# Attention's order on four engines: drawn by a builder that keeps a clock for each engine and counts buffers, in place of fixed rates

## The chip, the core and the metric

One core of a Trainium2 chip runs one kernel. It has five engines that follow their own instruction queues, each strictly in order, and wait for each other through semaphores: TensorE (PE; the loading of its weights is shown apart, as PEld), VectorE (DVE), ScalarE (ACT), GpSimd (POOL) and SyncE (SP), which here issues nearly all transfers. The metric is device time in microseconds (us), the median of the runs.

## What is computed

One layer of a streaming encoder on 1024 frames of width 1024: three token mixers side by side, merged by sigmoid gates, then a gated feed-forward block with a convolution. The two mixers whose order changes are both softmax attention over the whole sequence, eight heads each, in query blocks of 128:

```python
def one_block(args):
    i, q_blk = args
    s = jnp.einsum('bqhd,bkhd->bhqk', q_blk, k).astype(jnp.float32) * scale
    p = jax.nn.softmax(bias_mask(i, s), axis=-1).astype(v.dtype)
    return jnp.einsum('bhqk,bkhd->bqhd', p, v)
...
hn = rms_norm(x, norm_mix_g[l])
u = hn @ w_in[l]
...
y_a = mla_branch(...) @ w_br_mla[l]
y_b = fox_branch(...) @ w_br_fox[l]
y_c = ssm_branch(...) @ w_br_ssm[l]
g = jax.nn.sigmoid(u_gate + b_gate[l]).reshape(Bsz, S, N_BRANCH, D_MODEL)
merged = g[:, :, 0] * y_a + g[:, :, 1] * y_b + g[:, :, 2] * y_c
```

"mla" heads have keys of 96, "fox" heads keys of 64 and a decay added to the scores; both masks are causal, so query block i needs i + 1 key blocks. The third mixer is a state-space scan (SSD). Of the input projection u, the part for the SSD's convolution (12 blocks of 128 columns) and for the gates (24 blocks) is not computed ahead: it is kept back as filling work for TensorE.

## The kernel before

The program runs in stages, each a stretch of code in which the tile framework places semaphores by what every instruction reads and writes: projections and norms (about 0 to 384 us), attention (to 898 us), the SSD (to 1092 us), the three branch projections and the merge, the output projection, and the feed-forward block, which takes the last third of the time. Every product is done as three fp32r matmuls of high and low parts, which is why "h" and "l" tiles go in pairs.

**Attention.** A unit is two query rows (blocks of 128 queries, i = 2 jp and 2 jp + 1) of one head: 16 heads times 4 units. For a row, TensorE writes the scores `s` (L1303; for fox heads a small mask matmul L1313 closes them), VectorE takes the negated row maximum `nmx` (L1314), ScalarE the exponential with its sum `pm`, `rs` (L1316), VectorE the reciprocal (L1320), GpSimd multiplies the row by it (L1321). Then, for every pair of key blocks, TensorE transposes up to four blocks of `pm` into PSUM (`tp`, L1379), ScalarE copies them out as `pth` (L1384), VectorE subtracts to get `ptl` (L1385), and TensorE multiplies both by the values `vv` into one half of the accumulator `o` (PV, L1344 to L1352). The last PV of a unit is the narrow one on the diagonal. After it ScalarE copies one part of the half out (`o1`, L1357) and VectorE adds the other (`o2`, L1362), which is then stored. Units take the two halves of `o` in turn; both halves are one tile of 128 x 512 values.

**Fill.** `all_fill` yields the kept-back projection in grains of six matmuls of 512 columns (L1181, tile `mm`); a block of 128 columns is two halves of 24 matmuls. All halves use one PSUM bank, which ScalarE empties (L1159 for a gate, L1186 for a convolution block). Weights of a block are loaded one block ahead and split by ScalarE (`wh`, L1123) and VectorE (`wl`, L1124). A convolution block is followed by a chain on GpSimd (L1145), VectorE (L1138, six taps; L1142, two outputs) and ScalarE (L1151). What attention does not use of the fill is spent in the SSD, whose own budget per step is `FILL_SSD`.

**Who sets the order.** Within attention only TensorE is ordered by hand (`manual_schedule` with one engine). A builder merges three streams: the scores of unit n, the transposes and PV of unit n - 2, and fill at a fixed rate (`FILL_ATT` times the other work). Non-PE instructions are emitted by `later(us, fn)` when a single clock, which counts only TensorE's work, has passed a guessed delay; the PV stays two transposed blocks behind (`PVLAG`). The order on ScalarE, VectorE and GpSimd is then chosen by the framework's own scheduler, but for fill's instructions, which `pin` keeps in program order.

```python
later(t0 + 0.15, lambda: V.reduce_max(nmx[:, 0:1], row, axis=AX, negate=True))
t1 = t0 + 0.4 + 0.135 * n
pl[0] = later(t1, lambda: A.activation(p_[:, 0:n * P], row, AF.Exp, ...))
```

**Behind the SSD.** For its last chunk (the eighth) VectorE finishes `y`, ScalarE squares it, GpSimd and VectorE take the root, ScalarE scales it (L1597), TensorE transposes it in two groups (`stp`, L1605), which ScalarE copies out (`yT`, L1606). The branch projection starts with the fox branch (`ybr`, L1725) on `ah` and `al`, the split attention output (L134 on ScalarE, L135 on VectorE), whose first split is held behind the scaling of the last chunk.

Of the kernel before, what the change touches and what calls it, by code (L numbers as in the profile page):

```python
# [42 lines left out]
def block_kernel(ctx: ExitStack, tc: tile.TileContext, x, positions, norm_mix_g, w_in, b_gate,  # L43
# [1032 lines left out]
    def later(us, fn):  # L1076
        h = [clk[0] + us, uid(""), fn]
        queue.append(h)
        return h
# [9 lines left out]
    def force(h):  # L1089
        if h is not None and any(e is h for e in queue):  # L1090
            run_until(h[0])

    class Ring:


        def __init__(self, pool, shape, dt, tag, bufs):
            self.a = (pool, shape, dt, tag, bufs)
            self.last = []

# [12 lines left out]
    pin = tc.keep_in_program_order  # L1112

    def fill_load(c0, now=False):
# [8 lines left out]
        later(4.0, lambda: pin(A.activation(h, raw, AF.Copy)))  # L1123
        rl[0] = later(5.3, lambda: pin(V.tensor_sub(l, raw, f32(h))))  # L1124
        return h, l, rl

    def conv_done(j, u, ul, t0):
        a, al = f_t4.get()
        t = [t0]

        def step(us, fn):
            h = later(t[0], fn)
            t[0] += us
            return h
# [6 lines left out]
        def out(c0, c1):  # L1141
# [4 lines left out]
                                          op0=ALU.mult, op1=ALU.add))  # L1146
# [3 lines left out]
        for c0, c1 in ((0, 512), (512, S)):  # L1150
            step(1.6, lambda c0=c0, c1=c1: pin(A.activation(u[:, c0:c1], a[:, c0:c1], AF.Tanh)))  # L1151
        step(1.1, out(0, 512))
        al[0] = step(1.0, out(512, S))
        ul[0] = step(0.0, lambda: SY.dma_start(xbc_d[j], u))
# [8 lines left out]
    def all_fill():  # L1163
# [5 lines left out]
        for n, (kind, j, c0) in enumerate(blocks):  # L1169
# [3 lines left out]
            force(rl[0])  # L1173
            u, ul = f_t4.get()
            for half in range(2):
                f_half[0] += 1
                ps, pl = f_ps[f_half[0] % len(f_ps)].get()
# [12 lines left out]
                pl[0] = later(wait + 1.4, fn)  # L1190
                if half == 1:
                    if kind == "c":
                        conv_done(j, u, ul, 2.2)
                    else:
                        ul[0] = later(wait + 2.0, lambda u=u, g=g_d[kind][j]: SY.dma_start(g, u))
                t_h = clk[0]
                yield 0.65 * grain[0]
                for _ in range(4):
                    if len(f_ps) == 1 and clk[0] - t_h < 1.5 + 0.65 * grain[0]:
# [6 lines left out]
    def advance(gen):  # L1206
        c = next(gen, None)
        if c is not None:
# [79 lines left out]
    def score_row(o, i, pn):  # L1288
        flush()
        n = i + 1  # L1290
        chunks = row_chunks(i)
        p_, _ = a_pm.get()
        nmx, _ = a_nmx.get()
        rs, rl = a_rs.get()
        qs = slice(i * P, i * P + P)
        ps, pl = a_s.get()
        z = 512 - chunks[0][1] if len(chunks) == 2 else 0
        row = ps[:, z:z + n * P]
        for ci, (a, b) in enumerate(chunks):
            w = max(b - a, 256)  # L1300
            last = ci == len(chunks) - 1
            for i_, (q_, k_) in enumerate(o.passes):
                T.matmul(ps[:, z + a:z + a + w], q_[:, qs], k_[:, a:a + w], start=i_ == 0,  # L1303
                         stop=(o.br == 0 or not last) and i_ == len(o.passes) - 1)
            c = len(o.passes) * w / 2400
            if not last:
                yield c
        pn.append((p_, rl))

        def finish(t0=0.0):  # L1310

            if o.br == 1:
                T.matmul(row[:, n * P - P:n * P], identb, mfox, start=False, stop=True)  # L1313
            later(t0 + 0.15, lambda: V.reduce_max(nmx[:, 0:1], row, axis=AX, negate=True))  # L1314
            t1 = t0 + 0.4 + 0.135 * n
            pl[0] = later(t1, lambda: A.activation(p_[:, 0:n * P], row, AF.Exp, bias=nmx[:, 0:1],  # L1316
                                                   accum_out=rs[:, 0:1]))

            def norm():
                V.reciprocal(rs[:, 1:2], rs[:, 0:1])  # L1320
                G.tensor_scalar(p_[:, 0:n * P], p_[:, 0:n * P], rs[:, 1:2], 0.0, op0=ALU.mult, op1=ALU.add)  # L1321
# [888 lines left out]
```

## Time and profile before

| | |
|---|---|
| runs | 1999.05, 2001.5, 2002.47 us; median 2001.5 |
| profiled execution | 2000.52 us, its span 1998.8 us, granted clock 1.0 |
| attention, first fill matmul to last PV | 384.3 to about 898 us |
| SSD, to the first branch matmul | about 898 to 1092 us |
| fill matmuls in attention, in the SSD | 1195 and 533 of 1728, from the order of the instructions |

How to read it: PE's busy share counts pipelined matmuls whose ends are modelled, so two matmuls overlap in the rows; what one costs is the distance from its start to the next start. A view of waits names the engine that sat idle, the line it then ran, and the engine and line whose result came last.

### The profile page before, as it was taken

What the parts mean: (1) busy time and instruction counts of PE and PEld (TensorE: products, weight loads), DVE (VectorE), ACT (ScalarE), POOL (GpSimd) and SP (SyncE); (2) the same over time, 40 slices, a digit from 0 to 9 for tenths busy, and PEclk for the clock granted to TensorE, in tenths of its full rate; (3) what the DMA queues carried; (4) which work ended last, traced back from release to release, by engine and by line L of the source; (5) the groups of instructions that cost most, each with busy time, mean ns of one, the idle gap of its engine ahead of it and who ended that gap; (6) DMA issues with size and microseconds to landing.
All of it is one profiled execution on the core that took longest, in us unless ns stands there. A gap on an engine that the chain in (4) does not pass through costs nothing.

```text
span 1998.8 us, 28317 instructions
## 1 busy us (share of the span) xinstructions
PE 1975.3 (99%) x10185; PEld 1678.4 (84%) x10185; DVE 1340.1 (67%) x2153; ACT 929.3 (46%) x1650; POOL 660.1 (33%) x636
## 2 busy tenths in 40 slices
PE   8999999999999999999999999999999999999999
PEld 7989888888888888888888788888878888888887
DVE  7777567266656666656885476568998777665655
ACT  5555323255555555547775132225454445444432
POOL 5133322022222223213331262100664544523665
PEclk9999999999999999999999999999999999999999
DMA  5166857543535445427654786433332211249575
GB/s 179 52 195 211 276 178 226 166 126 105 139 114 146 116 124 134 127 78 238 182 193 137 258 278 211 139 125 104 107 95 85 76 61 49 79 154 336 195 259 193
DMA packets 278262, 312.15 MB, mean 156 GB/s; under 512 B 19197, under 2 KB 209289, under 8 KB 278122
## 3 DMA queue, kind: packets, MB, share of 16 engines
q1 hardware_dynamic: 278120, 310.35, 49.7%
q8 instruction: 80, 1.31, 0.3%
q14 instruction: 60, 0.49, 0.1%
q10 hardware_dynamic: 2, 0.00, 0.0%
HBM read 217.17 MB, written 93.13 MB: 155 GB/s over the span
## 4 chain that ended last, share of the span: by engine, by line
PE 88%; DVE 4%; DMA 3%; issue 2%; ACT 1%; POOL 1%; SPq 1%; ACTq 0%; DVEq 0%; POOLq 0%
PE mm L1181 18%; PE dn L2157 10%; PE fx L798 9%; PE ybr L1725 7%; PE ua L1816 6%; PE uc L1816 5%; PE ud L1816 4%; PE wo L1861 4%; PE s L1303 4%; PE tp L1379 3%; PE ub L1816 2%; PE fxv L188 2%; PE py L1570 1%; PE o L1352 1%; PE ckv L517 1%
## 5 line engine op out<-in xcount | busy, mean ns | idle before, releaser
L1321 POOL TENSOR_SCALAR pm<-pm,rs 128x128 f32<-128x128 f32 (+7 forms) x128 | 115.8, 906 | 403.0 <-DVE rs L1320 378.7
L1181 PE MATMUL mm<-hnh,wh 128*128 128x512 f32 x576 | 237.9, 413 | 0.0
L1181 PE MATMUL mm<-hnh,wl 128*128 128x512 f32 x576 | 225.9, 392 | 0.0
L1181 PE MATMUL mm<-hnl,wh 128*128 128x512 f32 x576 | 225.6, 392 | 0.0
L2157 PE MATMUL dn<-dr,dr 128*128 128x512 f32 x592 | 182.3, 389 | 0.0
L1385 DVE TENSOR_TENSOR ptl<-tp,pth 128x512 fp32r<-128x512 f32 (+1 forms) x160 | 98.7, 631 | 70.5 <-ACT pth L1384 69.9
L2157 PEld LDWEIGHTS dn<-dr,dr 128*128 128x128 f32 x592 | 111.1, 188 | 23.0
L1384 ACT ACTIVATE pth<-tp 128x512 fp32r<-128x512 f32 (+1 forms) x160 | 85.4, 555 | 94.5 <-PE tp L1379 94.3
L1181 PEld LDWEIGHTS mm<-hnh,wl 128*128 128x128 f32 x576 | 108.2, 188 | 24.8
L1316 ACT ACTIVATE pm<-s,nmx 128x128 f32<-128x128 f32 (+7 forms) x128 | 94.6, 741 | 71.8 <-DVE nmx L1314 71.3
L1314 DVE TENSOR_REDUCE nmx<-s 128x1 f32<-128x128 f32 (+7 forms) x128 | 95.3, 751 | 48.8 <-PE s L1303 26.9
L1181 PEld LDWEIGHTS mm<-hnl,wh 128*128 128x128 f32 x576 | 108.8, 189 | 15.9
L1181 PEld LDWEIGHTS mm<-hnh,wh 128*128 128x128 f32 x576 | 108.7, 189 | 16.1 <-DVE o L1362 0.2
L2157 PE MATMUL dn<-dr 128*128 128x512 f32 x296 | 115.2, 389 | 0.0
L135 DVE TENSOR_TENSOR dr<-dr,dr 128x1024 fp32r<-128x1024 f32 x52 | 71.5, 1382 | 52.1 <-ACT dr L134 48.1
L1725 PE MATMUL ybr<-ah,wl 128*128 128x512 f32 x256 | 99.7, 389 | 0.7 <-DVE wl L135 0.7
L1725 PE MATMUL ybr<-ah,wh 128*128 128x512 f32 x256 | 99.7, 389 | 0.3 <-ACT wh L134 0.3
L1725 PE MATMUL ybr<-al,wh 128*128 128x512 f32 x256 | 99.8, 390 | 0.0
L134 ACT ACTIVATE dr<-dr 128x1024 fp32r<-128x1024 f32 x52 | 55.1, 1061 | 71.7 <-PE dn L2157 51.0
L134 ACT ACTIVATE wh<-wr 128x1024 fp32r<-128x1024 f32 (+1 forms) x40 | 35.1, 877 | 97.8 <-PE ybr L1725 44.3
L1379 PE MATMUL tp<-ident,pm 128*128 128x128 f32 x576 | 79.1, 273 | 0.0
L135 DVE TENSOR_TENSOR wl<-S,wh 128x1024 fp32r<-128x1024 f32 x42 | 63.1, 1503 | 23.3 <-ACT wh L134 23.3
(528 smaller groups left out, 5705.3 us busy)
## 6 DMA issues: line engine op xcount, KB each, us to landing
dr<-act_d SPq DMA_DIRECT2D x99, 256.0 KB
wr<-in_w_in_dram SPq DMA_DIRECT2D x36, 512.0 KB
g_d<-t SPq DMA_DIRECT2D x24, 512.0 KB
gl<-g_d SPq DMA_DIRECT2D x24, 512.0 KB
wr<-in_ffn_w_up_dram SPq DMA_DIRECT2D x23, 512.0 KB
ws<-in_ffn_w_down_dram SPq DMA_DIRECT2D x22, 512.0 KB
wsum_d<-ws SPq DMA_DIRECT2D x22, 512.0 KB
act_d<-fa SPq DMA_DIRECT2D x22, 512.0 KB
```

The costliest lines, as they stand in the source:

```text
L134: i = A.activation(h, src, AF.Copy) if he is A else he.tensor_copy(h, src)
L135: return i, le.tensor_sub(l, src, f32(h))
L798: T.matmul(p, a(k), b(k), start=k == 0 and i == 0, stop=k == NK - 1 and i == 2)
L1181: T.matmul(ps, a[:, k, :], b[half][:, k, :], start=(k == 0 and i == 0), stop=(k == NK - 1 and i == 2))
L1314: later(t0 + 0.15, lambda: V.reduce_max(nmx[:, 0:1], row, axis=AX, negate=True))
L1316: pl[0] = later(t1, lambda: A.activation(p_[:, 0:n * P], row, AF.Exp, bias=nmx[:, 0:1], accum_out=rs[:, 0:1]))
L1321: G.tensor_scalar(p_[:, 0:n * P], p_[:, 0:n * P], rs[:, 1:2], 0.0, op0=ALU.mult, op1=ALU.add)
L1379: T.transpose(pt[:, off:off + P], pn[qi][0][:, k * P:k * P + P], ident)
L1385: pl[0] = later(cs + 0.6, lambda th=th, tl=tl, pt=pt, off=off: V.tensor_sub(tl[:, :off], pt[:, :off], f32(th[:, :off])))
L1725: T.matmul(pss[half], w_[:, k, :], a_[k][:, hs], start=k == 0 and i == 0, stop=k == nk - 1 and i == 2)
L1816: T.matmul(ps, a, b, start=first and n == 0, stop=n == 11, skip_group_check=not first)
L2157: T.matmul(ps[m], a[:, ts_], b[:, 512:], start=first_ and j == 0 and q == 0, stop=j == NFH - 1 and q == 2, skip_group_check=not first_)
```

## The change

It keeps all arithmetic and every number of instructions on each engine, and draws the order of attention anew. The builder now has a class `Task` (an engine, the time for which it blocks the engine, the time until its result is there, what it comes after, which buffers it takes) and a class `Sim`, with one clock for each of PE, ACT, DVE, POOL and the DMA queue. It places the task that can start first, an engine's ties by a rank; fill is put on TensorE when none of the three streams (PV before transposes before scores, `ORDER`) can start within `SLACK` of the end of the instruction before, or when fill is behind its share. A buffer's earlier owner must have been placed, and its end, plus `LATE`, counts. The costs are straight lines in the number of columns. Rows may now run as far ahead as the buffers allow (`pm` 8 buffers, was 6); the values need not be two blocks behind. A head's operands are loaded when the head two before it has ended. `manual_schedule` now holds PE, ACT, DVE and POOL, so their order in attention is the builder's, and `pin` does nothing there.

```diff
+    class Task:
+        def __init__(self, eng, cost, fn, after=(), est=0.0, order=(9, 0), rings=(), name=None):
+            self.eng, (self.pace, self.cost), self.fn = eng, cost, fn
...
-    pin = tc.keep_in_program_order
+    def pin(ins):
+        return ins if sim[0] is not None else tc.keep_in_program_order(ins)
...
-        later(4.0, lambda: pin(A.activation(h, raw, AF.Copy)))
-        rl[0] = later(5.3, lambda: pin(V.tensor_sub(l, raw, f32(h))))
+        i = later(4.0, lambda: pin(A.activation(h, raw, AF.Copy)), "A", (0.95, 1.06))
+        rl[0] = later(5.3, lambda: pin(V.tensor_sub(l, raw, f32(h))), "V", (1.13, 1.22), [i])
...
+    LATE = 0.09
+    class Sim:
...
+        def est(self, t):
+            if t.left:
+                return None
+            e = max([t.est] + [d.done + LATE for d in t.after])
+            for r, _ in t.rings:
+                if len(r.rel) >= r.bufs:
+                    o = r.rel[-r.bufs]
+                    if o.start is None:
+                        return None
+                    e = max(e, o.done + LATE)
+            return e
...
+        def pick_pe(self):
+            f = self.free["P"]
...
+            if t0 is not None:
+                behind = self.used < self.total * min(1.0, self.worked / self.work) + self.lead
+                if fe is None or (fe > t0 + 0.02 if behind else t0 < fe + SLACK):
+                    e = min((e for e in c if e[0] <= t0 + 0.02), key=lambda e: e[1])
+                    return e[0], e[2], e[3]
+            if fe is not None:
+                return fe, None, None
...
-    FILL_ATT = 1.08
+    ORDER = "VTS"
+    SLACK = 0.15
...
-        a_pm = Ring(atp, [P, S], F32, "pm", 6)
-        a_th, a_tl = (Ring(atp, [P, 512], F32R, n, PVLAG + 2) for n in ("pth", "ptl"))
+        PM, TH = 8, 4
...
-        with tc.manual_schedule(engines={mybir.EngineType.PE}):
...
-                merge(st, FILL_ATT * share)
...
+            m = Task("V", (d - 0.09, d), f_max, [ss[-1]], 0.0, (2, seq))
+            e = Task("A", (d - 0.115, d), f_exp, [m], 0.0, (2, seq), [(r_pm, last_t)])
+            rc = Task("V", (0.07, 0.16), lambda: V.reciprocal(r.rs[:, 1:2], r.rs[:, 0:1]), [e], 0.0, (1, seq))
+            d = 0.27 + 0.00084 * cols
+            r.norm = Task("G", (d - 0.025, d), lambda: G.tensor_scalar(...), [rc], 0.0, (1, seq))
...
+            o1 = Task("A", (0.27, 0.38), f_o1, (), 0.0, (0, seq))
+            o2 = Task("V", (0.33, 0.41), f_o2, [o1], 0.0, (0, seq))
...
+                h = Task("A", (d - 0.11, d), f_h, [t], 0.0, (1, seq))
+                l = Task("V", (d - 0.09, d), f_l, [h], 0.0, (0, seq))
+                v = Task("P", (c, c + 0.17), f_v, [l], 0.0, (0, seq), [(r_o, o2)] if kp == 0 else ())
...
+        with tc.manual_schedule(engines={mybir.EngineType.PE, mybir.EngineType.Activation, mybir.EngineType.DVE,
+                                         mybir.EngineType.Pool}):
+            work = 227.0
+            sm = Sim(fill, 268, work, 2.0)
```

What moves, at three places (in the rows, a name's numbers tell one buffer's use from the next).

TensorE, in the third unit of the fifth head: transposes (`tp`), fill (`mm`) and PV (`o`; `pth_1643` is made from `tp_1642`, and `pth_1594` from a `tp` well before these rows). Before:

```order
L1379 MATMUL tp_1642_6478<-ident_92,pm_1555_6311 128x128
L1379 MATMUL tp_1642_6478<-ident_92,pm_1567_6335 128x128
L1181 MATMUL mm_1609_6392<-hnh_1_118,wh_1509_6178 128x512
L1181 MATMUL mm_1609_6392<-hnl_3_120,wh_1509_6178 128x512
L1181 MATMUL mm_1609_6392<-hnh_1_118,wl_1510_6179 128x512
...
L1344 MATMUL o_4778<-pth_1594_6377,vv_1435_6008 128x256
L1346 MATMUL o_4778<-pth_1594_6377,vv_1435_6008 128x256
L1347 MATMUL o_4778<-ptl_1595_6378,vv_1435_6008 128x256
L1352 MATMUL o_4778<-ptl_1595_6378,vv_1435_6008 128x256
```

With the change, in the last unit of the fourth head, where `pth_1257` is made from `tp_1254`, just ahead of these rows, and `pth_1260` from the `tp_1259` that is seen here:

```order
L1587 MATMUL tp_1259_6265<-ident_92,pm_1219_6109 128x128
L1587 MATMUL tp_1259_6265<-ident_92,pm_1233_6165 128x128
L1599 MATMUL o_4778<-pth_1257_6261,vv_1113_5635 128x256
L1601 MATMUL o_4778<-pth_1257_6261,vv_1113_5635 128x256
L1602 MATMUL o_4778<-ptl_1258_6263,vv_1113_5635 128x256
L1607 MATMUL o_4778<-ptl_1258_6263,vv_1113_5635 128x256
L1203 MATMUL mm_1256_6254<-hnh_2_119,wh_1179_5910 128x512
L1203 MATMUL mm_1256_6254<-hnl_4_121,wh_1179_5910 128x512
L1203 MATMUL mm_1256_6254<-hnh_2_119,wl_1180_5911 128x512
...
L1599 MATMUL o_4778<-pth_1260_6274,vv_1113_5635 128x256
L1601 MATMUL o_4778<-pth_1260_6274,vv_1113_5635 128x256
```

Before, the PV of `tp_1642` stands 54 rows behind it; now that of `tp_1259` follows behind one other PV and six fill matmuls. By matmuls in between, each counted with its width, the median distance from a block's transposes to its PV falls to about a quarter.

VectorE, around the `o2` that closes the last unit of the fourth head (`t4` rows are convolution taps, `wl` the split of fill's weights). Before:

```order
L1138 SCALAR_TENSOR_TENSOR t4_1572_6353<-t4_1513_6180,pc_g_110,t4_1572_6353 128x512
L1320 RECIPROCAL rs_1591_6365<-rs_1591_6365 128x1
L1314 TENSOR_REDUCE nmx_1614_6417<-s_1616_6419 128x1
L1138 SCALAR_TENSOR_TENSOR t4_1572_6353<-t4_1513_6180,pc_g_110,t4_1572_6353 128x510
L1362 TENSOR_TENSOR o2_1618_6430<-o_4778,o1_1617_6429 64x256
L1124 TENSOR_TENSOR wl_1605_6390<-wr_1603_6387,wh_1604_6389 128x1024
L1314 TENSOR_REDUCE nmx_1631_6464<-s_1633_6466 128x1
```

With the change:

```order
L1595 TENSOR_TENSOR ptl_1258_6263<-tp_1254_6246,pth_1257_6261 128x512
L1595 TENSOR_TENSOR ptl_1261_6282<-tp_1259_6265,pth_1260_6274 128x512
L1595 TENSOR_TENSOR ptl_1266_6306<-tp_1262_6288,pth_1264_6296 128x384
L1595 TENSOR_TENSOR ptl_1267_6308<-tp_1263_6292,pth_1265_6304 128x384
L1571 TENSOR_TENSOR o2_1276_6338<-o_4778,o1_1268_6320 64x256
L1571 TENSOR_TENSOR o2_1278_6348<-o_4778,o1_1275_6336 64x256
L1534 TENSOR_REDUCE nmx_1279_6351<-s_1274_6332 128x1
```

Before, a row maximum and a tap stand ahead of `o2`; now it follows the `ptl` of its own unit and of the next one (`ptl_1267`, whose `o2_1278` comes right behind), and the row maximum comes after both.

TensorE at the end of the SSD, the last fill and the first branch matmuls. Before:

```order
L1181 MATMUL mm_3807_12459<-hnh_2_119,wl_3777_12309 128x512
L1181 MATMUL mm_3807_12459<-hnh_2_119,wh_3776_12308 128x512
L1181 MATMUL mm_3807_12459<-hnl_4_121,wh_3776_12308 128x512
L1181 MATMUL mm_3807_12459<-hnh_2_119,wl_3777_12309 128x512
L1725 MATMUL ybr_3831_12567<-ah_3815_12533,wh_3828_12561 128x512
L1725 MATMUL ybr_3831_12567<-al_3816_12534,wh_3828_12561 128x512
```

With the change:

```order
L1203 MATMUL mm_2717_12453<-hnl_4_121,wh_2667_12224 128x512
L1203 MATMUL mm_2717_12453<-hnh_2_119,wl_2668_12225 128x512
L1807 MATMUL stp_2720_12478<-ident_92,y_2665_12220 128x128 x4
L1807 MATMUL stp_2721_12484<-ident_92,y_2665_12220 128x128 x4
L1927 MATMUL ybr_2742_12567<-ah_2726_12533,wh_2739_12561 128x512
L1927 MATMUL ybr_2742_12567<-al_2727_12534,wh_2739_12561 128x512
```

Attention now takes 1222 fill matmuls and the SSD 506. Before, twelve fill matmuls stood between the last transposes (`stp`) and `ybr`, 72 between the last chunk's last other matmul (`py`) and `ybr`; now none and 36. On ScalarE the order there is the same in both: the two `yT` copies, then the first `ah`.

More of the change, by code (lines that the diff above doesn't have):

```diff
@@ L1286, in row_chunks @@
         return [(0, c * P), (c * P, n * P)]
[L1288 to L1321, printed above, removed]
-            rl[0] = later(t1 + 0.6 + 0.11 * n, norm)
-        if o.br == 0:
-            finish(c)
-            yield c
-        else:
-            held.append(finish)
-            yield c + 0.05
```

407 lines of the change are left out of this document (292 added, 115 removed).

## Prediction

> **What bounds the kernel now.** I read the page first, then attention and the SSD by windows, then the waits there, then the timeline at the longest wait and at the end of the SSD.
>
> ```profile
> PE 1975.3 (99%) x10185; PEld 1678.4 (84%) x10185; DVE 1340.1 (67%) x2153; ACT 929.3 (46%) x1650; POOL 660.1 (33%) x636
> PE 88%; DVE 4%; DMA 3%; issue 2%; ACT 1%; POOL 1%; SPq 1%; ACTq 0%; DVEq 0%; POOLq 0%
> 384.00:898.00 514.00, 510.14 (x3021) 440.28 (x3020) 316.65 (x600) 269.38 (x577) 129.92 (x140) 1.00 0.45 123
> 898.00:1092.00 194.00, 189.68 (x1052) 161.91 (x1051) 138.72 (x185) 135.14 (x282) 57.28 (x79) 1.00 0.58 184
> 384.00:898.00 514.00, 312.43 (x1195) 212.82 (x1195) 1.00 0.45 123
> 898.00:1092.00 194.00, 131.18 (x531) 97.24 (x532) 1.00 0.58 184
> 384.71 5.44 PE mm L1181 x24
> ```
>
> The first two rows are the page's busy times and its chain; the next two are attention and the SSD (length, then busy time of PE, PEld, DVE, ACT, POOL); then the same stretches for fill alone; the last is the chain's first piece in attention. TensorE is the bound: in attention it is busy 510 of 514 us at full clock, while VectorE has 197 us free, ScalarE 245 and GpSimd 384. A better order of these three engines is worth only what TensorE now waits for. Fill costs 5.44 / 24 = 0.227 us a matmul. As the number of matmuls is the same, TensorE's work can only change place.
>
> ```profile
> PEld o L1344 <- DVE o L1362: 4.5, 6, 2.7
> PE o L1344 <- DVE o L1362: 3.1, 3, 2.3
> PEld s L1303 <- ACT pm L1316: 0.9, 2, 0.7
> PE s L1303 <- ACT pm L1316: 0.5, 1, 0.5
> PEld tp L1379 <- DVE ptl L1385: 0.4, 2, 0.2
> 533.34 0.34 PE L1352 MATMUL o<-ptl,vv 128*128 128x256 f32 x1
> 534.28 1.05 ACT L1123 ACTIVATE wh<-wr 128x1024 fp32r<-128x1024 f32 x1
> 535.35 0.38 ACT L1357 ACTIVATE o<-o 64x256 f32<-64x256 f32 x1
> 535.80 1.22 DVE L1314 TENSOR_REDUCE nmx<-s 128x1 f32<-128x1024 f32 x1 [1.22 <-PE s L1303]
> 536.94 0.74 DVE L1138 SCALAR_TENSOR_TENSOR t<-t,pc_g,t 128x510 f32<-128x510 f32 x1
> 537.60 0.41 DVE L1362 TENSOR_TENSOR o<-o,o 64x256 f32<-64x256 f32 x1
> 538.06 0.38 PE L1344 MATMUL o<-pth,vv 128*128 128x256 f32 x1 [2.30 <-DVE o L1362]
> ```
>
> The waits of attention (us in total, times, longest): TensorE's main one is for `o2`, 3.1 us as PE's rows see it and 4.5 as the weight loads see it. The timeline shows the longest. The last PV of a unit started at 533.34; ScalarE first split weights, so `o1` ran at 535.35; VectorE had meanwhile gone to a row maximum whose scores were not yet there, then to a tap; `o2` ran at 537.60, and the next unit's first PV started 0.05 us behind its end. The work was ready; its order on ScalarE and VectorE made TensorE wait.
>
> **The change part by part.**
>
> *1. The waits that go.* `o1` and `o2` have the first rank now, and the scores' buffers and the PV are placed when the clocks say that they can start. PE's rows in this stage give 3.8 us (3.1, 0.5 and another 0.2 of `o1`), the weight loads' rows 5.8 or more (4.5, 0.9, 0.4). I take 5.2, nearer to the weight loads, since a late load of weights holds up its matmul too; ends 0 and 6.6. That they go is likely but not certain: the first PV of a unit needs the `o2` of the unit just before (the row at 538.06), while the planner counts two independent halves. In the new order 8 of 63 first PVs stand directly behind the unit before, but there they wait for ScalarE alone and `o2` waits for them; the next nearest have 1.4 us of TensorE's work between, and `o1` and `o2` take 0.38 + 0.41 with some 0.3 of hand-overs.
>
> *2. Fill that moves.* Attention takes 1222 fill matmuls in place of 1195: 27 x 0.227 = 6.1 us more here and 6.1 less in the SSD. By itself 0.
>
> *3. The cover at the end of the SSD.* Here the moved fill is missed.
>
> ```profile
> 1074.66 0.48 PE L1181 MATMUL mm<-hnh,wh 128*128 128x512 f32 x1
> 1081.48 1.15 ACT L1597 ACTIVATE y<-y,yr 128x1024 f32<-128x1024 f32 x1
> 1086.15 0.60 PE L1605 MATMUL stp<-ident,y 128*128 128x128 f32 x4
> 1089.37 0.60 PE L1605 MATMUL stp<-ident,y 128*128 128x128 f32 x4
> 1090.01 0.60 ACT L1606 ACTIVATE yT<-stp 128x512 f32<-128x512 f32 x1 [2.47 <-PE stp L1605]
> 1090.50 2.00 ACT L134 ACTIVATE ah<-ar 128x1024 fp32r<-128x1024 f32 x2
> 1091.58 2.36 DVE L135 TENSOR_TENSOR al<-ar,ah 128x1024 fp32r<-128x1024 f32 x2 [7.71 <-ACT ah L134]
> 1092.58 0.39 PE L1725 MATMUL ybr<-ah,wh 128*128 128x512 f32 x1
> 1092.86 0.50 PE L1725 MATMUL ybr<-al,wh 128*128 128x512 f32 x1
> ```
>
> Call T the first fill matmul behind the last `py` (1074.66). Before, 72 fill matmuls and three groups of transposes (about 0.44 each) led to `ybr` at T + 17.9. Now 36 matmuls and the same groups do, 8.2 + 1.3: TensorE is there at T + 9.5. The scaled `y` is there at 1082.63, T + 8.0, before the two last groups at T + 8.6. But then ScalarE has two copies of 0.6, and `ah` behind them by its order. The first copy starts 0.2 behind its group, about T + 9.3; the first `ah` ends near T + 11.6 and the first `al`, 1.2 long, at T + 12.85. `ybr`'s second matmul needs it, and in a run without waits it would start at T + 9.7. That is 3.1 us of waiting, where before some 0.2 was left: **+2.9**. The floor is 0, if other work came between (the order shows none); the ceiling 6.1, if all the moved fill was cover. Before, the twelve matmuls behind the last transposes hid these copies.
>
> *4. Waits that the closer order brings.*
>
> ```profile
> 512.31 1.04 PE L1379 MATMUL tp<-ident,pm 128*128 128x128 f32 x8
> 512.95 0.60 ACT L1384 ACTIVATE pth<-tp 128x512 fp32r<-128x512 f32 x1 [2.24 <-PE tp L1379]
> 513.58 0.69 DVE L1385 TENSOR_TENSOR ptl<-tp,pth 128x512 fp32r<-128x512 f32 x1 [0.51 <-ACT pth L1384]
> ```
>
> This is the bare hand-over from transposes to PV. The first four of eight are in by 512.75 (0.11 each), `pth` ends at 513.55 and `ptl` at 514.27: 1.5 us, 1.6 with the way back. Counting TensorE's work between a block's transposes and its PV, each instruction with the pitch that the timeline shows (fill 0.23, transposes 0.11, PV 0.12 or 0.06, scores 0.12 to 0.23), I get a median of 8.3 us before (shortest 3.0) and of 2.2 now (shortest 1.6). The PV's first two matmuls use only `pth`, which gives 0.24 more for `ptl`. So no PV stands nearer than the bare chain, but 36 of 160 have less than 0.6 us to spare, which is less than one `ptl` in front of them on VectorE. From a row's scores to its first transposes, the bare chain (maximum, exponential, reciprocal, multiplication) has at least 0.95 us to spare before, and now under 1 us in 11 of 128, under zero by 0.15 in two. The planner's costs have these very lengths (0.59 for that `pth`, 0.67 for `ptl`) and 0.09 for a hand-over where the rows show 0.03, so it errs a little to the safe side; and it counts TensorE no slower than the rows do. Ends: 0, and 36 x 0.3 = 11 us, if half an instruction more stood in front of each tight one. I take **2.0**, near the lower end, as the rows' lengths agree with the planner's.
>
> *Other edits at nothing.* Head operands come from a load one head ahead as before; its cover is that head's work, 514 / 16 = 32 us. More `pm` buffers only let rows run ahead. The SP queue starts attention with the same rows in the same order.
>
> The sum, on the profiled execution's own time: 2000.5 (its span 1998.8 and 1.7 around it) - 5.2 + 0 + 2.9 + 2.0 = **2000.2**. The median of the runs is 1.0 above that execution, so I forecast **2000**, and 1997.5 to 2004 as this case's own range.
>
> **The rivals.**
>
> *B, slower: the hand-overs are too close.* Place: ScalarE and VectorE between `tp` and PV. It decides when their queues hold one instruction more than the planner thought in front of a `pth` or `ptl`, since no later PV is there to be taken instead. For it: the distance fell from 8.3 to 2.2. Against: both engines have some 40% free, and lengths hardly scatter. Price: 11 in place of 2.0 gives 2009; with 5 more for rows, 2014.
>
> *C, faster: the SSD gains too.* These are TensorE's waits there before:
>
> ```profile
> PEld stp L1502 <- ACT E L1535: 1.6, 1, 1.6
> PEld stp L1502 <- issue: 1.6, 1, 1.6
> PEld stp L1502 <- PE stp L1605: 1.2, 1, 1.2
> PEld stp L1502 <- PE py L1570: 0.9, 1, 0.9
> ```
>
> All 5.3 us stand before the transposes of `x` (L1502) and none has a releaser that fits, so a transfer is meant. Its buffers come free with fill's blocks, whose places shift, and before the last `py` the SSD now has 9 fill matmuls more. Without 3 to 4 of these, and with a tail of 1 in place of 2.9: about 1994.5. Against: the loads' rules are unchanged, and a shift may add such waits.
>
> *D, the order does not remove the waits.* With part 1 at 0: 2005.4. For it: the shared accumulator; against: rank and order of `o2`.
>
> *E, GpSimd is held up, which the planner's fixed cost for it leaves out.*
>
> ```profile
> 499.42 0.92 POOL L1321 TENSOR_SCALAR pm<-pm,rs 128x768 f32<-128x768 f32 x1 [2.58 <-PE s L1303]
> 581.03 1.20 DVE L1124 TENSOR_TENSOR wl<-wr,wh 128x1024 fp32r<-128x1024 f32 x1
> 581.28 1.99 POOL L1321 TENSOR_SCALAR pm<-pm,rs 128x384 f32<-128x384 f32 x1 [4.70 <-DVE rs L1320]
> 582.16 0.74 DVE L1138 SCALAR_TENSOR_TENSOR t<-t,pc_g,t 128x510 f32<-128x510 f32 x1
> ```
>
> Half the columns took twice as long, and the multiplication ended 0.37 us behind two VectorE instructions that ran back to back. In the new order 23 of 128 reciprocals have such an instruction right behind them (33 before), up to 2.7 us of them in a row (before 2.0). Their transposes stand further away than the delay in each case, by 0.07 us in the closest, so I count 0; if half of their 21 us (each run of instructions less the 0.25 that the multiplication starts behind it) showed, 2000.2 + 10.5 = 2010.7. [...]
>
> **How the numbers follow.** Chances: the forecast 0.52, B 0.15, C 0.20, D 0.08, E 0.05. A difference under 0.2% (4 us, 1997.5 to 2005.5) cannot be told from no change. Of the forecast's 0.52, 0.05 falls below and 0.03 above that; all of C is faster; B is slower but for 0.03, D for half, E whole. So faster 0.25, same 0.51, slower 0.24. The range 1993.5 to 2009 leaves out about half of B, E, and a third of C.
>
> **What would show it.** Part 1: the waits of PE for `o2` (3.1) near 0, and attention at 514 + 6.1 - 5.2 + 2 = 517 us. Part 2: 1222 fill matmuls before the last PV. Part 3: PE waits of about 3 us for `ah` and `al` at the first `ybr`, and an SSD stage of 194 - 6.1 + 2.9 = 191. Part 4: PE waits for `ptl`, `pth` or `pm` that sum to about 2. The forecast is wrong if these sum to 8 or more, if attention falls under 513, or if the SSD keeps its length or loses more than 5.

## The result and the profile after

The changed kernel takes 2014.81 us (median; 2012.93 to 2016.63), the kernel before 2001.99 on the same chip: a ratio of 1.0065, 95% interval 1.0052 to 1.0077. It is slower by some 13 us, where 2000 was forecast and 2009 was the end of the range. The profiled executions are 16.1 us apart (spans 2014.9 and 1998.8); that of the changed kernel is the slowest of its four runs, so the stages below add up to some 3 us more than the medians differ by.

The first row is the page's busy times of the changed kernel. Then comes the view by windows, cut at the first scores, the last PV and the first branch matmul (`ybr`): length, then busy time of PE, PEld, DVE, ACT and POOL, granted clock, share of the DMA engines, GB/s. First the changed kernel:

```profile
PE 1984.3 (98%) x10185; PEld 1683.6 (84%) x10185; DVE 1345.1 (67%) x2153; ACT 933.5 (46%) x1650; POOL 666.0 (33%) x636
388.92:903.41 514.49, 512.53 (x3023) 440.68 (x3021) 318.48 (x599) 275.42 (x577) 127.13 (x140) 1.00 0.45 123
903.41:1103.63 200.22, 188.05 (x1026) 160.19 (x1024) 139.15 (x185) 133.02 (x281) 62.86 (x79) 0.97 0.56 175
1103.63:2014.90 911.27, 902.38 (x3988) 744.65 (x3988) 630.22 (x657) 368.71 (x444) 366.14 (x220) 1.00 0.47 156
```

and the kernel before:

```profile
389.99:898.08 508.09, 504.24 (x2995) 435.42 (x2994) 315.96 (x599) 268.78 (x576) 129.92 (x140) 1.00 0.45 123
898.08:1092.58 194.50, 190.18 (x1053) 162.29 (x1052) 139.30 (x185) 135.64 (x282) 57.28 (x79) 1.00 0.58 185
1092.58:1998.80 906.22, 899.09 (x3989) 742.08 (x3987) 625.53 (x657) 368.46 (x443) 365.42 (x220) 1.00 0.47 156
```

Attention is 6.4 us longer; 6.1 of it is the fill that moved in (1198 matmuls here against 1171, without the 24 ahead of the first scores). The SSD has 27 fill matmuls fewer and is 5.7 us longer all the same: 11.9 us worse than its work. The rest, which the change does not touch, is 5.1 us longer. And the clock, 1.00 in every stretch before, is 0.97 in the SSD.

The waits of TensorE in the changed kernel, first in attention, then from the last PV to 1170 us (us in total, times, longest):

```profile
PE tp L1587 <- POOL pm L1547: 1.1, 2, 0.7
PE mm L1203 <- ACT t L1180: 0.8, 2, 0.5
```

```profile
PE stp L1704 <- DMA t<-xbc_d: 5.3, 1, 5.3
PE stp L1704 <- issue: 2.9, 1, 2.9
PE ybr L1927 <- ACT ah L134: 1.7, 1, 1.7
PE mm L1203 <- ACT t L1180: 1.7, 1, 1.7
PE ybr L1927 <- DVE wl L135: 1.1, 1, 1.1
PE ybr L1927 <- ACT wh L134: 0.8, 1, 0.8
PE ybr L1927 <- DVE al L135: 0.8, 1, 0.8
```

and in the kernel before, from its last PV to 1160 us:

```profile
PE stp L1502 <- issue: 1.4, 1, 1.4
PE stp L1502 <- DMA t<-xbc_d: 1.2, 1, 1.2
...
PE ybr L1725 <- DVE wl L135: 0.7, 1, 0.7
PE ybr L1725 <- ACT wh L134: 0.3, 1, 0.3
```

In attention the waits for `o2` are gone, and none for `pth` or `ptl` has come. The large waits stand behind attention. Two of them lie at the start of the SSD. The timeline there (start, length, engine, line; in brackets the idle time before and what ended it):

```profile
903.78 0.38 ACT L1567 ACTIVATE o<-o 64x256 f32<-64x256 f32 x1 [5.26 <-PE o L1607]
904.06 1.04 ACT L1142 ACTIVATE wh<-wr 128x1024 fp32r<-128x1024 f32 x1
905.13 0.69 ACT L1180 ACTIVATE t<-mm,pc_g 128x512 f32<-128x512 f32 x1
905.87 0.50 PE L1203 MATMUL mm<-hnh,wh 128*128 128x512 f32 x1 [1.67 <-ACT t L1180]
...
916.81 0.33 SPq L1220 DMA_DIRECT2D g_d<-t  x1
918.87 0.42 SPq L1690 DMA_DIRECT2D t<-xbc_d  x1
926.73 1.09 PE L1704 MATMUL stp<-ident,t 128*128 128x128 f32 x4 [5.34 <-DMA t<-xbc_d]
```

*The gate.* Behind attention fill has a second PSUM bank, and its halves take the two in turn. Attention now ends with the first half of a block; the next half falls to the bank that this one has just filled, and TensorE waits for the gate that empties it, which ScalarE runs behind `o1` and a split. Before, the half that began there had the new bank, and TensorE's starts show a delay of less than 0.1 us.

*The load of x.* The block that is half done at the end of attention holds one of the four `t4` buffers until its gate is stored (916.81). The second chunk's `x` goes into such a buffer, stands behind that store on SyncE and is issued at 918.87; before, it was issued at 906.04, behind a block that ended 1 us after attention, and TensorE waited 1.2 us for it.

*The end of the SSD* and *the clock* are below. By the distances of TensorE's starts, the 16.1 us are: -1.1 ahead of attention; +0.3 in attention beside the fill; 1.8 for the gate; 4.2 more for `x`; 2.9 more at the first two `ybr`; 7.5 for matmuls that ran at half clock; 0.5 for the rest. In the rest are waits that grew and others that shrank: those for `wl` and `wh` at the branch, near 1161 us, are 1.0 us longer than before.

### The profile page after: what moved, and what is told of

It is laid out like the page before. It is cut to its first block, busy times and chain, and to the rows that moved or that the text cites. A ratio compares the mean times of both kernels' runs of the same rounds, so it can differ in the third digit from the quotient of the medians.

```text
span 2014.9 us, 28350 instructions
## 1 busy us (share of the span) xinstructions
PE 1984.3 (98%) x10185; PEld 1683.6 (84%) x10185; DVE 1345.1 (67%) x2153; ACT 933.5 (46%) x1650; POOL 666.0 (33%) x636
## 4 chain that ended last, share of the span: by engine, by line
PE 89%; DVE 3%; DMA 3%; issue 2%; ACT 1%; POOL 1%; SPq 1%; ACTq 0%; DVEq 0%; POOLq 0%
PE mm L1203 19%; PE dn L2359 10%; PE fx L798 9%; PE ybr L1927 7%; PE ua L2018 6%; PE uc L2018 5%; PE ud L2018 4%; PE wo L2063 4%; PE s L1520 4%; PE tp L1587 3%; PE ub L2018 2%; PE fxv L188 2%; PE py L1772 1%; PE o L1607 1%; PE q L188 1%
```

## What the runs showed of the clock

In the trace of before the clock is 1.00 from 12 us to the last microsecond. In the changed kernel, ahead of its last 1.4 us, four stretches run at 0.50. The first, by windows (columns as above):

```profile
917.85:921.27 3.42, 3.42 (x19) 2.83 (x17) 1.87 (x3) 3.42 (x8) 1.33 (x1) 1.00 0.87 247
921.27:924.68 3.41, 0.12 (x2) 0.00 (x0) 3.41 (x2) 2.20 (x4) 3.41 (x2) 1.00 1.03 343
924.68:928.09 3.41, 1.36 (x6) 1.30 (x7) 3.38 (x5) 0.19 (x1) 0.97 (x1) 0.50 1.06 353
928.09:931.51 3.42, 3.42 (x10) 2.65 (x9) 2.17 (x4) 0.41 (x1) 0.00 (x0) 0.50 0.19 58
931.51:934.92 3.41, 3.41 (x16) 2.79 (x15) 1.38 (x2) 1.14 (x2) 0.00 (x0) 1.00 0.31 129
```

TensorE is busy for 0.12 of 3.41 us in the second window, the clock is 0.50 from that window's end (924.68), and it is back at 1.00 at 931.51, behind one window in which TensorE was busy throughout. In the fourth row ten matmuls take the window that sixteen take in the fifth. The other stretches, from 992.95, 1105.59 and 1163.62, are 3.41 us long, and all the borders lie on one grid: 20, 33 and 17 windows of 3.413 us apart. Each window at 0.50 with full work costs 1.6 to 1.7 us, the long stretch 2.6; together 7.5.

The windows ahead of the four stretches have TensorE busy for 0.03, 0.35, 0.35 and 0.44 of their length. Their waits are the one for `x`, the one of 2.9 us, those for `ah` and `al`, and those for `wh` and `wl`. The last is not the order's alone: two kernels below have the same order of TensorE there (useless matmuls, and the early load of x in the changed kernel), waited 0.2 us or less for `wh`, and have no such stretch. With the 1.0 us by which these two waits grew, some 2.6 of the 16.1 us need not be the change's.

So the waits were counted by the window into which they fell. Cutting the 14 profiled executions of this study, from 12 to 1985 us, into such windows (8078 of them) and taking PE's busy share in each: all 22 with less than 0.45 were followed by a window at 0.50. Of the eleven between 0.45 and 0.55 three were. Above 0.55 there was one, and that one was at 0.50 already. The busy shares count modelled ends, so these counts put the edge between 0.45 and 0.55 and no sharper. The kernel before has one window in there and none below. It is the one with the 2.3 us wait for `o2`, busy 1.82 of 3.41 or 0.53, and the next one ran at 1.00:

```profile
533.94:537.35 3.41, 1.82 (x8) 1.13 (x6) 2.19 (x4) 1.77 (x4) 1.02 (x1) 1.00 0.67 169
```

In one experiment below (the early load in the old order) the same wait fell differently on the grid, left its window at 0.33, and cost 1.6 us more by TensorE's starts.

In the changed kernel no single wait had to fill a window: those of 1.7 and 0.8 us for `ah` and `al` left TensorE busy for 1.19 of 3.41 us from 1102.18 to 1105.59, and that was enough for the stretch behind it.

## The experiments

Theory P: the order in attention is about as good as the old one, and the time is lost because the SSD starts at another place in fill's blocks and ends with less fill, and because the waits that follow lower the clock. Theory O: the new order itself, or what it leaves on ScalarE and VectorE, costs the time. "Beside fill" is a stage's length less 0.227 us for each of its fill matmuls.

| kernel | median us | ratio to before, 95% | attention beside fill | SSD beside fill | rest | windows at 0.50 |
|---|---|---|---|---|---|---|
| before | 2000.5 to 2002.0 | 1 | 242.3 | 73.5 | 906.2 | 0 |
| changed | 2014.8 | 1.0065 (1.0052 to 1.0077) | 242.5 | 85.4 | 911.3 | 5 |
| fill's total 263 | 2008.9 | 1.0042 (1.0027 to 1.0057) | 245.0 | 79.3 | 907.9 | 1 |
| before, fill rate 1.11 | 2013.4 | 1.0066 (1.0051 to 1.0081) | 247.7 | 78.8 | 909.0 | 2 |
| fill's total 256 | 2015.4 | 1.0075 (1.0060 to 1.0090) | 247.9 | 83.6 | 906.7 | 3 |
| useless matmuls in a wait | 2012.4 | 1.0058 (1.0042 to 1.0075) | 242.6 | 83.7 | 908.4 | 3 |
| same SSD (total 262) | 2002.8 | 1.0008 (0.9999 to 1.0018) | 245.1 | 72.4 | 906.6 | 0 |
| a block less (251) | 2003.7 | 1.0011 (1.0002 to 1.0021) | 244.0 | 74.4 | 906.4 | 0 |
| a block more (273) | 2014.6 | 1.0069 (1.0052 to 1.0086) | 246.7 | 79.0 | 912.2 | 3 |
| same SSD, GpSimd priced higher | 2003.8 | 1.0013 (1.0003 to 1.0022) | 243.3 | 75.3 | 907.4 | 1 |
| same SSD, fewer switches | 2005.3 | 1.0016 (1.0008 to 1.0025) | 244.5 | 75.5 | 911.0 | 3 |
| the same, total 261 | 2004.3 | 1.0014 (1.0005 to 1.0023) | 247.2 | 72.3 | 907.2 | 1 |
| changed, early load of x | 2009.4 | 1.0045 (1.0031 to 1.0058) | 242.6 | 81.7 | 910.5 | 3 |
| before, early load of x | 2003.0 | 1.0013 (1.0004 to 1.0021) | 243.8 | 73.5 | 908.5 | 1 |

The stages and the windows are those of the profiled execution of each, which can lie some us from the median (5.4 above it in the first run with fewer switches). In four of them one window at 0.50 stands at 40 us, ahead of everything that was edited: totals 256 and 261, the useless matmuls, and the run with fewer switches at 262.

**Less fill in the new order, more in the old.**

```diff
-            sm = Sim(fill, 268, work, 2.0)
+            sm = Sim(fill, 263, work, 2.0)
```

> The changed kernel with the planner's fill total at 263 in place of 268, nothing else: attention then takes 1196 fill matmuls (24 of them ahead of the first scores) where the changed kernel takes 1222 and the kernel before 1195, and the SSD begins at the place in fill's blocks where it began before. Theory P (the loss comes from the place: attention now ends half a block further on in fill, so that at the start of the SSD TensorE waits for the gate of the one mm bank, the second load of x waits for that block's store, and the end of the SSD has less cover; the long gaps then lower TensorE's clock): attention 508 us, SSD about 194, no stretch at clock 0.5, 1999 to 2001 us in all. Theory O (the new order of ScalarE and VectorE is what costs, wherever fill stands): still 2010 or more.

```diff
-    FILL_ATT = 1.08
+    FILL_ATT = 1.11
```

> The kernel before with fill's rate in attention at 1.11 in place of 1.08, nothing else: attention takes 1220 fill matmuls in place of 1195 and ends half a block further on, in the old order. Theory P: the changed kernel's SSD returns in the old order: the wait of 1.7 us for a gate right behind attention, a wait of some 5 us at the second group of x, 36 fill matmuls for the tail, two or more stretches at clock 0.5; 2009 to 2014 us. Theory O: 2000 to 2003.

The old order with more fill is as slow as the changed kernel, 2013.4. Some 5 us of that are lost in attention, whose pauses over 0.3 us grow from 4.7 to 10.3 us in sum, and the others behind it: 0.8 us for a gate and 2.8 for the load of `x` at the start of the SSD, 3.2 at the first `ybr`, two stretches at half clock. (The view puts the 2.8 us down to a gate on ScalarE that ended at 931.4; but the load, issued at 925.48 behind the store of another gate, landed at 931.39, and the transposes of `x` began at 931.53.) So an order need not be new to lose this. The new order with less fill came back by 5 to 6 us only, to 2008.9, which is the number of neither theory. Its TensorE has 1196 fill matmuls ahead of the last PV, one more than before, but the count that matters is the builder's, where the SSD's own merge begins: there it stands at 1182, with half block 50 begun, while the old builder stands at 1176, the end of half block 49. From there on the two merges deal out fill in other places, and the SSD waits 7.8 us at `stp` and `pst` instead of 4.3. The kernels with a total of 262 make that count equal.

**The end of a block.** The same edit with 256.

> The changed kernel with the planner's fill total at 256: attention takes 1152 fill matmuls, which is 24 whole blocks of 48, so the SSD starts on a new block; 576 are left for it (506 in the changed kernel, 533 before), 108 of them behind the last py. Theory P: no wait for a gate at the boundary, the second load of x is not late, no wait at ybr; 1997 to 2001. If instead attention needs the fill as cover, its waits rise above the 2.7 us of the changed kernel by some us and the time is 2003 or more. Theory O: 2010 or more.

The number, 2015.4, is in theory O's range, but the run does not test what it was meant to. The count of 24 whole blocks was again taken from TensorE's order; the builder stood at 1140, half block 48 begun. The SSD's start has a load of `x` that is late by 1.5 us and a wait of 2.7 for `xddl`, and attention lost 5 us more. The run says only that a longer tail alone does not help; what tells the theories apart are the next runs.

**The same SSD.**

```diff
-            sm = Sim(fill, 268, work, 2.0)
+            sm = Sim(fill, 262, work, 2.0)
...
+            owed[0] = 0.4144
             merge([], 6.0)
```

> The changed kernel with fill's total at 262 and the SSD's merge begun with the 0.4144 us owed that the kernel before has there: the program of attention ends after 1176 fill matmuls, 49 half blocks, as before, and from its first transposes to ybr the SSD has on TensorE the same order as before, to the matmul; the orders of ScalarE, VectorE and SyncE there differ from before over its first two chunks only. Theory P (the SSD lost its place in fill, and attention's own order is as good as the old one): SSD 193 to 196 us, no wait of TensorE there above 2.5, no stretch at clock 0.5, 1999 to 2002 us. Theory O (what attention's new order leaves on ScalarE and VectorE costs the SSD, or attention itself is slower): 2006 or more.

The same with 251 and with 273 in place of 262:

> As the run with fill's total at 262, but with 251: attention takes one block of 48 fill matmuls less (47 half blocks), the SSD keeps its order, with 60 fill matmuls in place of 12 behind its last transposes. Theory P: the phase is the same, so the time is that run's within 2 us unless attention misses the cover; its waits then show that (up to 5 us more). If any shift of fill out of attention costs, 2006 or more.

> As the run with fill's total at 262, but with 273: one block of 48 more in attention (51 half blocks, the phase of before), so the SSD begins as before and only its end has less: 24 fill matmuls behind the last py in place of 72, none behind the last transposes. Theory P, both parts: no wait at the start of the SSD, but TensorE reaches ybr some 11 us earlier than before and waits there: by the rows of before the operands stand 12.9 us behind the last py, TensorE comes about 6.8 behind it, so 6 us of waits and one stretch at clock 0.5 (1.7): 2006 to 2009. If the tail needs no cover: 2000 to 2002.

This decides between P and O. With the new order in attention and the SSD begun at the old place, the time is that of before within 0.2%, and there is no window at 0.50. One block less in attention, at the same place in a block, changes nothing. The order in attention is not free, though: beside its fill attention takes 2.8 us more than before in the run with 262, and 1.7 more with 251. TensorE's waits from 894 to 1170 us in the run with 262:

```profile
PE stp L1704 <- issue: 2.5, 2, 1.4
PE ybr L1928 <- DVE wl L135: 1.1, 1, 1.1
PE stp L1704 <- PE py L1772: 0.8, 1, 0.8
```

One block more has the right place too, and its SSD starts well, but 24 fill matmuls are too few for the end:

```profile
PE ybr L1928 <- ACT ah L134: 3.2, 1, 3.2
PE stp L1807 <- ACT y L1799: 1.7, 1, 1.7
...
PE ybr L1928 <- DVE al L135: 0.5, 1, 0.5
```

By TensorE's starts that is about 6.3 us of waits, as the 6 expected; it was not expected that two windows in a row would then run at 0.50, and one more at 1161 us (4.3 us together). It ends at 2014.6, and 4.4 us of that are in attention beside its fill. The end of the SSD alone thus cost some 9 us here (the waits and the two windows), and the SSD begun at another place in fill some 6 in the run with 263; the changed kernel has some of both.

**The clock by itself.** The results of these matmuls are overwritten; nothing is left out.

```diff
                 pt = psp.tile([P, 512], F32, name=uid("stp"), tag="tp", bufs=2)
+                if c == 1 and g == 0:
+                    for _ in range(22):
+                        T.matmul(pt, hnh[0][:, 0, 0:P], hnh[0][:, 0, :], start=True, stop=True)
```

> The changed kernel with 22 useless matmuls (22 x 0.227 = 5.0 us, results overwritten) ahead of the transposes of x of the second chunk, which wait 5.3 us for their load; TensorE waits as long but is busy. If the stretch at clock 0.5 from 924.7 to 931.5 us comes from TensorE's idle time, it vanishes and the time falls by 2 to 3 us to about 2012; the wait itself stays. If the clock does not follow TensorE's idle time, the stretch stays and the time is that of the changed kernel, 2015, or a little more.

```profile
922.31 5.28 PE L1705 MATMUL stp<-hnh 128*128 128x512 f32 x22
928.43 0.66 PE L1707 MATMUL stp<-ident,t 128*128 128x128 f32 x4 [0.84 <-DMA t<-xbc_d]
```

As expected: the load comes no earlier, but the clock stays at 1.00 behind it, and by TensorE's starts 1.7 us are won at this place. In the changed kernel this idling was paid a second time after the wait was over (2.6 us at half clock), and here work that does nothing avoided it. The median falls from 2014.8 to 2012.4, but against the kernel before on the same chips that is +12.8 and +11.4 us, with intervals that overlap: the medians alone do not show it. The stretches at 992 and 1105 us stayed; that at 1163 is missing too, which this edit does not explain.

**The load of x.**

```diff
             load_xs(obj[0], 0)
+            load_xs(obj[1], 1)
             load_rows(obj[0], 0)
...
-            if c + 1 < NT:
+            if 0 < c and c + 1 < NT:
                 load_xs(obj[c + 1], c + 1)
```

> The changed kernel with the load of x for the SSD's second chunk issued with the first chunk's, ahead of the SSD's first fill, in place of inside the first chunk: on SyncE it then stands ahead of attention's last store and no longer behind the store of the gate whose block attention left half done. TensorE's order is the same. If that queue place is what made the 5.3 us wait, the wait vanishes and with it the stretch at clock 0.5 behind it (6.8 us long, 2.7 lost): 2014.8 - 5.3 - 2.7 = about 2007, with the gate's wait, the wait at ybr and the other stretches left. If the buffer or another engine made it, the wait only changes its name and the time is 2012 or more.

> The kernel before with the same early load. There TensorE waited 1.37 us more than its pitch for that load (at 914.6 us). Without it 1 to 1.5 us less, 2000 against 2001.3; if the earlier load holds up attention's last store or the chunk's other loads, no change.

In the changed kernel both loads are now issued at 887 us, and the wait of 5.3 us is gone, so SyncE's queue and the buffer behind it made it. The median falls by 5.4 us (against before on the same chips from +12.8 to +9.0), not 8; by TensorE's starts 3.7 are won at this place. The chain continues, and the next instruction that needs the chunk waits.

```profile
PE stp L1704 <- issue: 2.9, 1, 2.9
PE pst L1746 <- DVE xddl L135: 2.1, 1, 2.1
```

That leaves its window at 0.38, and one window at 0.50 (926.0) remains of two. The edit is not a gain in the old order: its wait of 1.4 us at 914 us is gone, another at 952 grew from 1.1 to 2.0, and the wait for `o2` at 533 us met the grid as told above.

**What attention still loses.**

```diff
-            d = 0.27 + 0.00084 * cols
+            d = 0.77 + 0.00084 * cols
             r.norm = Task("G", (d - 0.025, d), ...
```

> As the run with fill's total at 262, with the planner's price of GpSimd's multiplication raised by 0.5 us for all 128; the SSD keeps the same order on all engines. In the changed kernel two multiplications took twice their length beside VectorE's work and TensorE waited 1.1 us for them. If those delays are what attention still loses, its waits for pm vanish and the time is 1 to 2 us below that run; if the larger distance only pushes other work together, the same or more.

The delay itself is real. In the changed kernel this multiplication took 1.93 us beside two taps of VectorE; the row of before with the same 768 columns took 0.92. TensorE waited for it in the middle of eight transposes:

```profile
535.16 1.38 DVE L1158 SCALAR_TENSOR_TENSOR t<-t,pc_g,t 128x512 f32<-128x512 f32 x2
535.40 1.93 POOL L1547 TENSOR_SCALAR pm<-pm,rs 128x768 f32<-128x768 f32 x1 [4.28 <-DVE rs L1545]
537.38 0.98 PE L1587 MATMUL tp<-ident,pm 128*128 128x128 f32 x7 [0.71 <-POOL pm L1547]
```

But a higher price for all 128 does not cure it: the waits for `pm` were 0.2 us in the run with 262 and are 0.9 here. Attention is 1.8 us shorter beside fill, and the SSD 2.9 longer, with one window at 0.50. Its order is the same on every engine but ScalarE, where the trace has four of 282 instructions in other places, near the SSD's start. The median does not fall.

Another loss was thought to be one that no wait shows. Two rows of scores of one shape in the changed kernel, the first behind PV, the second behind transposes:

```profile
409.90 0.86 PE L1520 MATMUL s<-w0h,w0l 104*128 104x512 f32 x3
410.60 0.39 PE L1203 MATMUL mm<-hnh,wh 128*128 128x512 f32 x1
...
435.89 0.60 PE L1587 MATMUL tp<-ident,pm 128*128 128x128 f32 x4
436.25 0.94 PE L1520 MATMUL s<-qk,qk 104*128 104x512 f32 x3
437.03 0.40 PE L1203 MATMUL mm<-hnh,wh 128*128 128x512 f32 x1
```

From their starts to the next: 0.70 and 0.78 us. In both traces, wherever transposes or a mask end and other matmuls begin, the first of these holds TensorE about 0.089 us longer (a fill matmul behind transposes 0.316 us, by the median, where one costs 0.227). The old order has 136 such places in attention, the new one 177, because it seldom takes two blocks of transposes in a row, or transposes behind a mask (24 times before, 3 now): by this count 12.4 and 15.7 us in all, so 3.4 more.

But the count sees one side of the change only. The four transposes in the rows above take 0.36 us from their start to the scores, where four at their distance of 0.109 would take 0.44: behind the last of a block the next matmul starts after 0.03 us. With both sides counted, the changes behind transposes cost 0.8 us in all before and 0.9 now, which is nothing. Behind a mask some of it is real: the mask and what follows take about 0.05 us more than with transposes behind it, and over all masks that is 1.1 us more in the new order. A rule was added to the planner by the first count:

```diff
+            if self.last in ("T", "M"):
+                for e in c:
+                    if e[3] == "T" and e[0] <= f + 0.3:
+                        return e[0], e[2], "T"
             t0 = min([e[0] for e in c], default=None)
```

> As the run with fill's total at 262 (the SSD as before), with one rule more in the planner: behind transposes, or behind a mask, the next transposes go first if they can start within 0.3 us. In the traces so far a matmul behind transposes or a mask holds TensorE 0.089 us longer than elsewhere; the old order of attention has 136 such places, the new one 176 or 177, this one 145. If that is what the new order's attention gives back, its loss falls by 31 x 0.089 = 2.8 us: 1997 in the profiled execution, 2000 in the median. If these 0.089 us are hidden elsewhere, the time stays at 2002.8.

> The same rule at fill's total of 261: a second order of attention with 144 such places and the same SSD. It tells the rule from the luck of one order: 2000 again if the rule is what counts, and otherwise anything from 1999 to 2005, as the waits of attention fall.

The places fell to 145 and 144 and their cost by the first count to 12.8 and 12.9 us, as expected. The time did not follow. With both sides counted there was little to win, as only 11 or 12 of the places that went stand behind a mask (0.6 us), and pauses over 0.3 us in attention rose from 3.4 us to about 4 and 7, for `pm`, for the scores' buffers and once, for 1.7 us, for a gate. Attention beside fill is 244.5 and 247.2, against 245.1. The 2000 expected of this rule was not reached, and of all the kernels tried none beats the one before.

## Why the prediction was wrong

**What bounds the kernel.** Right, with one thing left out: TensorE is the bound, but its clock was taken as given because it was 1.00 throughout. No term and no rival had a price for the clock; it is 7.5 of the 16.1 us in the profiled execution, 1.6 of them at the stretch that the order alone does not make.

**Step 1, the waits that go, and step 4, waits of the closer order.** Right in kind. The waits for `o2` in PE's rows are zero, so rival D is out. New waits were put at 2.0, for `ptl`, `pth` or `pm`; they are 1.1 for `pm` and 0.8 for a gate in fill's one bank. Rival B, too, is out: no PV waited for its operands, so a median distance of 2.2 us is enough. Together -3.2 was forecast. The 5.2 of step 1 was more than all pauses over 0.3 us that TensorE's starts show before, 4.7; these went to 2.7. About 1.1 us came back behind the masks, a term that the sum did not have, and about as much in delays under 0.3 us that no run separates: +0.3 with all else. The change's own gain was real and was spent inside attention.

**Step 2, fill that moves: "by itself 0".** This is the step that failed. The matmuls do cost the same at full clock (in the trace of before the next one starts 0.231 us behind a fill matmul in attention and 0.230 in the SSD, by the median), but fill comes in blocks of 48 with buffers, banks, gates and loads, and the SSD's start depends on where in a block it begins. 27 matmuls are half a block and a little more. That turned the bank, put a store in front of a load, and cost 1.8 + 4.2 us and the first stretch at half clock, 2.6 more: 8.6 of the 16.1 us. With the SSD back on its old place in fill, start and end, the time is 2002.8. The prediction weighed this, for the faster side alone, in rival C; its "a shift may add such waits" was what happened.

**Step 3, the cover at the end of the SSD.** Right to the tenth of a microsecond in its own terms. T is 1092.09 in the trace, the first fill matmul behind the last `py`; the second `ybr` was forecast at T + 12.85:

```profile
1103.63 0.49 PE L1927 MATMUL ybr<-ah,wh 128*128 128x512 f32 x1 [1.73 <-ACT ah L134]
1104.89 0.50 PE L1927 MATMUL ybr<-al,wh 128*128 128x512 f32 x1 [0.76 <-DVE al L135]
```

It started at T + 12.80, and the loss by starts is 1.9 + 1.0 = 2.9, as forecast. What is missing is what this wait sets off: TensorE was busy for 0.35 of that window, and the next one ran at 0.50, for 1.6 us more. The run with a block more shows the same step at its full size.

**Rival E.** The delay of GpSimd's multiplication was there (1.93 us beside two taps, against 0.92), at 1.1 us of TensorE's waits for `pm` where 0 was counted and 10.5 named as its price. What makes it slow beside VectorE's work, no run shows.

**The stages.** Attention was forecast at 517 us, counted from the first fill matmul (383.5 here): it is 519.9. The SSD was forecast at 191: it is 200. The prediction said that it would be wrong if the SSD kept its length or lost more than 5; it did neither, it grew.

Left open: the 2.9 us before the transposes at 991.75 us have no releaser in the trace; the copy out of their PSUM buffer ended 0.3 us earlier, behind ScalarE's eight rows for `E`, which suggests ScalarE's order, but no run separates it. Nor is it settled why the SSD takes 72.3 to 75.5 us beside fill in four runs with the same order on TensorE, VectorE, GpSimd and SyncE. On ScalarE they fall into two pairs: 262 and 261 with fewer switches (72.4 and 72.3) have one order, the higher price and 262 with fewer switches (75.3 and 75.5) another, by four places. The longer pair has a window at 0.50 in it (at 956 and 958 us, 1.6 us of it), behind a wait of 2.0 and 2.3 us for the transposes of `x` that is 1.1 and 1.0 in the shorter; that the four places make this wait is not shown.

## What to carry to other kernels

When a change moves filler work across a stage border, count it in the filler's own unit, and look at what the half-done unit holds there: its bank, its buffer, its place in the transfer queue. On an engine that is the bound, price a wait by the window it falls into: in the changed kernel short waits that together left TensorE busy for 0.35 to 0.44 of a window of 3.41 us cost another 1.6 to 1.7 us each time, and at the wait for `x` useless matmuls avoided the stretch at half clock. And compare two orders with everything behind them held equal, as the runs with the same SSD do; otherwise a difference of half a per cent says nothing of the order.
